# The last feed-forward product of a two-layer trunk: features on the partitions, or tokens

## The chip, the cores and the metric

The kernel runs on one core of one Trainium2 chip. The metric is the device time of one execution in microseconds; lower is better. Five engines work beside each other: TensorE (PE; PEld is its load of the stationary operand), VectorE (DVE), ScalarE (ACT), GpSimd (POOL) and SyncE (SP, which here issues loads and stores). Each runs its own queue in order and waits for others by semaphores.

## What is computed

The reference is a two-layer decoder trunk on x of 256 tokens by 1024 features, all in float32. Cut to what matters here, its end:

```python
h = modulate(rms_norm(x, norm_g[1, 2]), sh3, sc3)
g, u = jnp.split(h @ ffn_w_in[1, 1], 2, axis=-1)          # 1024 -> 2 x 2816
x = x + 0.5 * g3[:, None, :] * ((silu(g) * u) @ ffn_w_out[1, 1])   # 2816 -> 1024
return rms_norm(x, final_g)
```

Ahead of it stand three more such feed-forward blocks, a differential attention and a forgetting attention, which the change leaves alone.

## The kernel before

x lies in SBUF with features on the partitions: tile `xx`, 128 partitions x 8 blocks of features x 256 tokens. Every weight is streamed from memory by SP in pieces of up to 1024 columns into six `raw` buffers; ACT rounds a piece to the matmul's format (`wh`, `cp_part`, line 286), DVE takes the rest (`wl`, `sub_part`, line 296), into six and five buffers. Each product is three matmuls: high by high, low by high, high by low (`mm3`, line 396: the weights are the loaded operand and the activations stream, 256 columns). `v_proj` (line 717) has it the other way round: activations loaded for each half of the tokens, weights streamed, 512 columns.

The order of the work is written out by the program: a planner (`InOrder`, line 55) keeps an estimated clock for each engine, and `bg`, `fill_act` and `fill_dve` put the pieces' casts and subtractions between the other instructions as buffers come free. `later`, `run_laters` and `flush` (lines 381 to 394) put work off by so many steps of the loop.

The block at the end is `ffn(1, 1, "late", ..., None)`. Its first loop over j = 0 to 10 computes 256 hidden features at a time into PSUM banks pg and pu; `evac` makes silu(g) * u and splits it into `hidh` and `hidl`, 22 blocks of 128 features by 256 tokens in all. Its second loop goes over n = 0 to 7, a block of 128 output features each: 22 x 3 matmuls into one bank `po`, then `x_update` (line 417): DVE adds gate times po to x[n], ACT squares it and multiplies it by final_g, and DVE sums the squares over n. After the last n, `rstd_of` (line 446) sums over the partitions with a matrix of ones (two matmuls into psn), takes the reciprocal root on ACT and refines it in three DVE steps; four DVE products scale x, two feature blocks each, and SP and ACT store them in turn (lines 1245 to 1250). The output leaves as 128 x 8 x 256, and the host turns it round. `need` (line 225) makes sure that a column of the conditioning (shift, scale, gate; the `ada` products on DVE) has been computed.

Of the kernel before, what the change touches and what calls it, by code (L numbers as in the profile page):

```python
# [10 lines left out]
F32 = mybir.dt.float32  # L11
# [3 lines left out]
ALU = mybir.AluOpType  # L15
# [31 lines left out]

V_NORM = 0
V_KVN = 48
V_FIN = 56  # L50
V_SUB = 64
V_ADAB = 65

# [51 lines left out]
def trunk(ctx, tc, a, out):  # L105
# [54 lines left out]
    def table(func):  # L160
        act.preload_act_table(func)
# [74 lines left out]
    def add_ffn(l, i):  # L236
        if (l, i) == (0, 0):
            stream.extend((a["win0"][k], K0 * 512, 1024) for k in range(NC))
        n = 2 * (NG - K0 if (l, i) == (0, 0) else NG)
        stream.extend((a["win"][win0_of(l, i) + u], 2048, 1024) for u in range(n))  # L240
        stream.extend((a["wout"][(2 * l + i) * 16 + u], 11 * P, 768) for u in range(16))

    add_ffn(0, 0)
    stream += [(a["wqk"][u], 2048, 1024) for u in range(2)]
# [146 lines left out]
    def flush():  # L391
        for e in laters[:]:
            laters.remove(e)
            e[1]()
# [22 lines left out]
    def x_update(n, ps, gate, nxt, acc_eng):  # L417

        dve.scalar_tensor_tensor(x[n], ps, gate[:, n:n + 1], x[n], op0=ALU.mult, op1=ALU.add)
        hh, hl = hn[n]
        if nxt is not None:
            A = mods[nxt[0]][1]
            act.activation(hh, x[n], AF.Copy, scale=A[:, n:n + 1])
        sq = kp.tile([P, S], F32, tag="sq", name=f"sq{n}")
        act.activation(sq, x[n], AF.Square)
        if nxt is None:
            y = xx
            act.activation(y[:, n], x[n], AF.Copy, scale=vecs[:, V_FIN + n:V_FIN + n + 1])  # L430

        def second():
            if nxt is not None:
                dve.scalar_tensor_tensor(hl, x[n], A[:, n:n + 1], hh.bitcast(F32),
                                         op0=ALU.mult, op1=ALU.subtract)
# [94 lines left out]
    def ffn(l, i, kind, m, nxt, at=2):  # L530
# [93 lines left out]
        for j in range(j0, NG):  # L624
            pg, pu = mmbank(f"pg{j}"), mmbank(f"pu{j}")
            for kh in range(2):
                blk = take("win")
                for kk in range(4):
                    k = kh * 4 + kk
                    for b in range(4):  # L630
                        mm3((pg, pu)[b // 2][:, (b % 2) * 256:(b % 2) * 256 + 256],
                            blk(kk * 512 + b * P), hn[k], k == 0 and b % 2 == 0, k == NC - 1)
                    run_laters()
            evac(pg, pu)
            if (l, i) == (0, 0) and j == K0 + 2:
                constants()
        table(AF.Abs_reciprocal_sqrt)
        gate = (l, 2 if i == 0 else 8)
        for n in range(NC):
            po = mmbank(f"po{n}")[:, :S]  # L640
            if n == NC - NFILL:
                mode[0] = "fill"
            for hf in range(2):
                blk = take("wout")
                for kk in range(11):
                    k = hf * 11 + kk
                    if n == 0 and k == 18:
# [8 lines left out]
            if nxt is not None:  # L656
                need(nxt[0]) if n >= 4 else None
            if n == NC - 1 and nxt is not None:
                need(*nxt)
                shift_cols(nxt)  # L660

            def upd(n=n, po=po):
                f = x_update(n, po, mods[gate][1], nxt, dve)
                later(1, f)
            if n < NC - 1:
                later(1, upd)
            else:
                flush()
                flush()
                upd()  # L670
                flush()

    class OutProj:

# [342 lines left out]
    ffn(0, 1, "late", ((0, 7), (0, 6)), (("kv", 1), ("kv", 0)), at=3)  # L1017


    kT = [cp_.tile([P, 512], F32, name=f"kT{j}") for j in range(4)]  # L1020
    vb = [[cp_.tile([P, 512], F32, name=f"vb{t}{nh}") for nh in range(2)] for t in range(2)]
# [223 lines left out]
    y = xx  # L1245
# [27 lines left out]
def _layout(x, c, ada_w, ada_b, norm_g, ffn_w_in, ffn_w_out, a_w_qkv, a_w_o, a_lambda,  # L1273
# [56 lines left out]
    r["wout"] = ffn_w_out.reshape(4, 2, 11, P, NC, P).transpose(0, 4, 1, 3, 2, 5).reshape(64, P, 11 * P)  # L1330

    def vmat(w):
        return w.reshape(2, 4, P, 2, 512).transpose(3, 0, 2, 1, 4).reshape(4, P, 2048)
# [42 lines left out]
```

## Time and profile before

| | us |
|---|---|
| median of 3 runs | 989.79 (988.62 to 990.39) |
| the profiled execution | 990.28 |
| its span, first to last instruction | 988.5 |
| PE busy | 974.5 (99%) |
| DVE, ACT, POOL busy | 807.1, 561.4, 63.3 |
| first loop of the last block, from about 807; second loop | to 918.49; 918.49 to 978.35 |
| from the last po matmul to the span's end | 10.15 |

The profile is of one execution. A matmul's own duration (0.28) is modelled to its last result; the pace is read from start to start or from the length of a chain of matmuls. Engines' busy shares are averages over stages with different limits, so a stage is read by its own stretch.

### The profile page before, as it was taken

The page shows a single profiled execution, that of the slowest core. Times are in us where ns is not written, and L with a number is a line of the kernel's source. Part 1 is how long each engine was busy: PE and PEld are TensorE (multiplying, and loading weights), DVE is VectorE, ACT ScalarE, POOL GpSimd, SP SyncE. Part 2 cuts the span into 40 slices and gives each one's busy share as a digit, 9 for nine tenths or more (in the row PEclk, how much of TensorE's full clock was granted, in tenths as well). Part 3 has the DMA queues.
Part 4 walks back from the last instruction along what each step waited for, and adds up shares of the span by engine and source line. Part 5 has one row for each costly group of instructions (what it writes and reads, how often), then busy time and mean ns, then how long its engine had stood idle before and what let it go on. Part 6 is the DMA issues. An engine that isn't in the chain of part 4 may idle for free. (4 is left out here: it accounts for less than half of the span.)

```text
span 988.5 us, 20569 instructions
## 1 busy us (share of the span) xinstructions
PE 974.5 (99%) x8168; PEld 949.6 (96%) x8168; DVE 807.1 (82%) x1329; ACT 561.4 (57%) x923; POOL 63.3 (6%) x88
## 2 busy tenths in 40 slices
PE   8999999999999999999999999999999999999996
PEld 7999999988999999999998999999998999999996
DVE  6989879989899998788897988889986697555553
ACT  4465545575877644555575544445567676554552
POOL 0000100000112000000100000000047110000000
PEclk9999999999999999999999999999999999999998
DMA  9987999958766699889957999989765237554551
GB/s 361 414 336 277 338 363 332 364 205 303 271 226 234 227 383 362 302 266 314 337 185 301 342 343 332 331 289 342 256 226 173 84 117 256 197 194 144 176 177 43
DMA packets 67570, 265.07 MB, mean 268 GB/s; under 512 B 7785, under 2 KB 7937, under 8 KB 57362
## 3 DMA queue, kind: packets, MB, share of 16 engines
q1 hardware_dynamic: 65376, 258.31, 72.8%
q0 software_dynamic: 1664, 4.81, 1.7%
q8 instruction: 64, 1.05, 0.4%
q10 hardware_dynamic: 434, 0.64, 0.2%
q14 instruction: 32, 0.26, 0.1%
HBM read 262.66 MB, written 2.65 MB: 268 GB/s over the span
## 5 line engine op out<-in xcount | busy, mean ns | idle before, releaser
L100 DVE TENSOR_TENSOR wl<-raw,wh 128x1024 fp32r<-128x1024 f32 (+1 forms) x368 | 401.6, 1106 | 95.0 <-issue 24.9
L100 ACT CAST wh<-raw 128x1024 fp32r<-128x1024 f32 (+1 forms) x368 | 349.1, 958 | 205.3 <-PE pu L100 98.8
L100 DVE CUSTOM_DVE_ANT_0 ada<-ada,cact,vecs 128x1024 f32<-128x1024 f32 x160 | 203.5, 1279 | 0.2 <-DMA ada<-in_ada 0.2
L100 PE MATMUL po<-hidl,wh 128*128 128x256 f32 x704 | 194.4, 276 | 0.2 <-DVE hidl L100 0.2
L100 PE MATMUL po<-hidh,wh 128*128 128x256 f32 x704 | 194.4, 276 | 0.0
L100 PE MATMUL po<-hidh,wl 128*128 128x256 f32 x704 | 194.3, 276 | 0.0
L100 PE MATMUL pg<-HH,wl 128*128 128x256 f32 x608 | 168.2, 277 | 0.0
L100 PE MATMUL pg<-HH,wh 128*128 128x256 f32 x608 | 168.2, 277 | 0.0
L100 PE MATMUL pu<-HH,wh 128*128 128x256 f32 x608 | 168.1, 277 | 0.0
L100 PE MATMUL pu<-HL,wh 128*128 128x256 f32 x608 | 168.1, 276 | 0.0
L100 PE MATMUL pg<-HL,wh 128*128 128x256 f32 x608 | 168.0, 276 | 0.0
L100 PE MATMUL pu<-HH,wl 128*128 128x256 f32 x608 | 168.0, 276 | 0.0
L100 PEld LDWEIGHTS po<-hidl,wh 128*128 128x128 f32 x704 | 132.1, 188 | 0.4 <-DVE hidl L100 0.4
L100 PEld LDWEIGHTS po<-hidh,wh 128*128 128x128 f32 x704 | 132.2, 188 | 0.0
L100 PEld LDWEIGHTS po<-hidh,wl 128*128 128x128 f32 x704 | 132.2, 188 | 0.0
L100 PEld LDWEIGHTS pg<-HH,wh 128*128 128x128 f32 x608 | 114.1, 188 | 0.7 <-ACT hidh L100 0.6
L100 PEld LDWEIGHTS pg<-HL,wh 128*128 128x128 f32 x608 | 114.2, 188 | 0.0
L100 PEld LDWEIGHTS pg<-HH,wl 128*128 128x128 f32 x608 | 114.2, 188 | 0.0
L100 PEld LDWEIGHTS pu<-HH,wh 128*128 128x128 f32 x608 | 114.2, 188 | 0.0
L100 PEld LDWEIGHTS pu<-HL,wh 128*128 128x128 f32 x608 | 114.2, 188 | 0.0
L100 PEld LDWEIGHTS pu<-HH,wl 128*128 128x128 f32 x608 | 114.2, 188 | 0.0
L100 ACT ACTIVATE HH<-ht,modall 128x256 fp32r<-128x256 f32 x56 | 28.0, 508 | 39.9 <-DVE ht L100 38.0
(215 smaller groups left out, 1627.5 us busy)
## 6 DMA issues: line engine op xcount, KB each, us to landing
raw<-in_win SPq DMA_DIRECT2D x176, 512.0 KB, 6.1
ada<-in_ada SPq DMA_DIRECT2D x79, 1024.0 KB, 7.5
raw<-in_wout SPq DMA_DIRECT2D x64, 384.0 KB, 5.1
raw<-in_wout SPq DMA_DIRECT2D x64, 320.0 KB, 4.7
raw<-in_wqk SPq DMA_DIRECT2D x16, 512.0 KB, 5.4
raw<-in_wo SPq DMA_DIRECT2D x16, 512.0 KB, 5.0
raw<-in_wv SPq DMA_DIRECT2D x8, 512.0 KB, 7.2
raw<-in_wkk SPq DMA_DIRECT2D x8, 512.0 KB, 8.5
```

What stands on the lines that cost most here:

```text
L100: return self.tc.keep_in_program_order(f(*args, **kw))
```

## The change

The second loop of the last block is written anew, with its norm and its stores (class `Last`); the other three blocks keep theirs. Tokens now lie on the partitions. For each quarter of the output features (256), two banks are filled, one for each half of the tokens: `hid` is the loaded operand, 128 tokens wide, and the split weights stream, 256 columns. The weights come from a new array `wlast` with the same numbers in that order, in pieces of 1024 and 768 columns, each at an offset of 32 columns in its buffer. In the last quarter the first eight blocks are done for both halves, then the other fourteen for the first half of the tokens, its update and its store, and then the same for the second half.

So x has to be turned. In the first loop, at j = 1, DVE transposes all of x in squares of 32x32 into the tile `turned`; at j = 2 to 9 POOL issues four DMAs each, 32 in all, that put the squares into place in x's own tile (runs of 32 floats). At j = 6 POOL writes the gate to memory and reads it back as a row on all partitions, and reads final_g likewise. The tiles of the forgetting attention's keys and values are joined into two tiles whose room `turned` and `rows` take over. The sum of squares is now along the free dimension, on DVE with each quarter, and the root is a power on POOL over one column. The output leaves as 128 x 2 x 1024.

```diff
+    shift.update({p: 32 for p, v in enumerate(pieces) if v[0].tensor is a["wlast"].tensor})
...
             evac(pg, pu)
...
+            if nxt is None:
+                last.between(j)
+        if nxt is None:
+            last.down(hid)
+            return
         table(AF.Abs_reciprocal_sqrt)
...
+        def between(self, j):
+            if j == 1:
+                self.turned = cp_.tile([P, NC, 2, 4, 32], F32, tag="kT", name="turned")
+                for k in range(0, NC, 2):
+                    dve.transpose(self.turned[:, k:k + 2].rearrange("p k h b j -> p (k h b j)"),
+                                  xx[:, k:k + 2].rearrange("p k t -> p (k t)"))
+            elif 2 <= j < 10:
+                for fb, tb in self.moves[2 * j - 4:2 * j - 2]:
+                    to = self.x[tb * 32:tb * 32 + 32].rearrange("p h (k b j) -> p h k b j", k=NC, b=4)
+                    for h in range(2):
+                        nc.gpsimd.dma_start(to[:, h, :, fb], self.turned[fb * 32:fb * 32 + 32, :, h, tb])
+            if j == 6:
+                need(self.gate)
+                g = mods[self.gate][1]
+                gdram = tc.dram_tile([1, D], F32, name="gdram")
+                nc.gpsimd.dma_start(bass.AP(gdram.tensor, gdram.offset, [[1, P], [P, NC]]), g)
+                self.rows = cp_.tile([P, 2, D], F32, tag="vb", name="rows")
+                nc.gpsimd.dma_start(self.rows[:, 0], bass.AP(gdram.tensor, gdram.offset, [[0, P], [1, D]]))
+                nc.gpsimd.dma_start(self.rows[:, 1], bass.AP(a["fin"].tensor, a["fin"].offset, [[0, P], [1, D]]))
+
+        def update(self, t, q, po):
+            cs = slice(q * 256, q * 256 + 256)
+            xs = self.x[:, t, cs]
+            m = kp.tile([P, 256], F32, tag="sq", name=f"m{t}{q}")
+            dve.tensor_tensor(m, po, self.rows[:, 0, cs], op=ALU.mult)
+            dve.tensor_tensor(xs, m, xs, op=ALU.add)
+            j = kp.tile([P, 256], F32, tag="ht", name=f"j{t}{q}")
+            s = self.sums[:, 8 * t:8 * t + 8]
+            dve.tensor_tensor_reduce(j, xs, xs, 1.0, 0.0, ALU.mult, ALU.add, accum_out=s[:, q:q + 1])
...
+            elif q == 3:
+                dve.tensor_scalar(s[:, 6:7], s[:, 3:4], 1.0 / D, s[:, 5:6], op0=ALU.mult, op1=ALU.add)
+                nc.gpsimd.tensor_tensor(s[:, 7:8], s[:, 6:7], half[:, :1], op=ALU.pow)
+            if q < 3:
+                dve.tensor_tensor(xs, xs, self.rows[:, 1, cs], op=ALU.mult)
+
+        def store(self, t):
+            r = self.sums[:, 8 * t + 7:8 * t + 8]
+            y = self.x[:, t]
+            act.activation(y[:, :512], y[:, :512], AF.Copy, scale=r)
+            act.dma_start(out[:, t, :512], y[:, :512])
+            dve.scalar_tensor_tensor(y[:, 768:], y[:, 768:], r, self.rows[:, 1, 768:], op0=ALU.mult, op1=ALU.mult)
+            dve.tensor_scalar(y[:, 512:768], y[:, 512:768], r, None, op0=ALU.mult)
+            sp.dma_start(out[:, t, 512:], y[:, 512:])
+
+        def down(self, hid):
+            def part(po, t, k, w):
+                hh, hl = hid[k // 2]
+                o = (k % 2) * 256 + t * P
+                wh, wl = w
+                mm(po, hh[:, o:o + P], wh, start=k == 0, stop=False)
+                mm(po, hh[:, o:o + P], wl, start=False, stop=False)
+                mm(po, hl[:, o:o + P], wh, start=False, stop=k == 21)
+                work(P)
+            mode[0] = "fill"
+            for q in range(4):
+                po = [mmbank(f"po{q}{t}")[:, :256] for t in range(2)]
+                for u in range(3 if q < 3 else 1):
+                    blk = take("wlast")
+                    for kk in range(8 if u < 2 else 6):
+                        k = 8 * u + kk
...
+                        w = blk(kk * 256, 256)
+                        for t in range(2):
+                            part(po[t], t, k, w)
+                        run_laters()
+                if q < 3:
+                    for t in range(2):
+                        later(1 + t, lambda t=t, q=q, po=po: self.update(t, q, po[t]))
+            flush()
+            blks = [take("wlast", True) for _ in range(2)]
+            for t in range(2):
+                for k in range(8, 22):
+                    part(po[t], t, k, blks[(k - 8) // 8](k % 8 * 256, 256))
+                self.update(t, 3, po[t])
+                self.store(t)
...
+    last = Last(1, (1, 8))
     ffn(1, 1, "late", ((1, 7), (1, 6)), None, at=3)
-    y = xx
-    r = rstd_of()
-    rb = r.rearrange("p (o t) -> p o t", o=1).to_broadcast([P, 2, S])
-    for k in range(0, NC, 2):
-        dve.tensor_tensor(y[:, k:k + 2], y[:, k:k + 2], rb, op=ALU.mult)
-        (sp, act)[k // 2 % 2].dma_start(out[:, k:k + 2], y[:, k:k + 2])
...
+    r["wlast"] = w[3].reshape(22, P, 4, 256).transpose(2, 1, 0, 3).reshape(4, P, 22 * 256)
```

## Rows read from the trace of the kernel before

**Rows 1.** The page's busy time by engine, and TensorE's granted clock in 40 slices of the span, in tenths of full speed.

```profile
PE 974.5 (99%) x8168; PEld 949.6 (96%) x8168; DVE 807.1 (82%) x1329; ACT 561.4 (57%) x923; POOL 63.3 (6%) x88
...
PEclk9999999999999999999999999999999999999998
```

**Rows 2.** Busy time by stretch. The columns are the stretch and its length, busy us and instructions of PE, PEld, DVE, ACT and POOL, the granted clock, the DMA share and GB/s. A stretch of an earlier block, the last block's first loop, its second loop, and the end.

```profile
330.00:400.00 70.00, 70.00 (x619) 70.00 (x618) 65.88 (x87) 36.02 (x41) 0.00 (x0) 1.00 0.93 347
...
829.00:918.00 89.00, 89.00 (x788) 89.00 (x787) 48.41 (x49) 43.34 (x50) 0.00 (x0) 1.00 0.56 183
918.50:978.40 59.90, 59.90 (x530) 59.86 (x529) 31.16 (x44) 28.63 (x43) 0.00 (x0) 1.00 0.45 136
978.40:988.50 10.10, 1.06 (x4) 0.30 (x2) 4.29 (x8) 1.40 (x3) 0.00 (x0) 0.66 0.28 104
```

**Rows 3.** The chain that ended last, in order of time, from 915 us on: start, length, engine and tile.

```profile
918.49 59.86 PE po L100 x528
...
978.37 0.49 DVE x L100
...
980.60 0.49 DVE ra L100
...
981.12 0.44 DVE ra L100
...
982.04 0.69 DVE x L100
```

**Rows 4.** The queues of SP and ACT at the end (start, time from the first issue to the end of the last), and the output's tile: issue times in ns, and time from issue to landing.

```profile
982.76 1.58 SPq L100 DMA_DIRECT2D out<-x  x2
983.37 1.61 ACTq L100 DMA_DIRECT2D out<-x  x2
...
L100 ACTq DMA_DIRECT2D out<-x x2: 350/350/350, 983.4 to 984.6; - x2
...
DMA to landing us min/median/max: 2.4/2.5/2.6
```

**Rows 5.** TensorE's pace. The chain from 786 us on: seventy-two pw matmuls of 256 columns, and groups of six of the first loop of the last block at two lengths. Then from TensorE's timeline the first and the last of seventeen rows, each the first of three 512-column matmuls of v_proj.

```profile
788.25 8.57 PE pw L100 x72
...
811.42 0.71 PE pu L100 x6
812.13 0.68 PE pg L100 x6
...
528.40 0.39 PE L100 MATMUL pv<-wh,HH 128*128 128x512 f32 x1
...
539.39 0.39 PE L100 MATMUL pv<-wh,HH 128*128 128x512 f32 x1
```

**Rows 6.** Groups of instructions by line, engine, operation, tiles and shapes: busy us, mean ns of one, idle time before them.

```profile
L100 DVE TENSOR_TENSOR wl<-raw,wh 128x1024 fp32r<-128x1024 f32 x240 | 289.8, 1222 | 57.5 <-issue 19.9 <-ACT sg L100 14.9 <-PE pu L100 10.5
...
L100 DVE CUSTOM_DVE_ANT_0 ada<-ada,cact,vecs 128x1024 f32<-128x1024 f32 x160 | 203.5, 1279 | 0.2 <-DMA ada<-in_ada 0.2
...
L100 ACT ACTIVATE sq<-x 128x256 f32<-128x256 f32 x48 | 19.5, 406 | 14.6 <-DVE x L100 13.7 <-POOL acc L440 1.0
...
L100 DVE SCALAR_TENSOR_TENSOR x<-po,modall,x 128x256 f32<-128x256 f32 x32 | 15.3, 479 | 7.4 <-PE po L100 7.3
...
L100 DVE TENSOR_TENSOR acc<-acc,sq 128x256 f32<-128x256 f32 x20 | 8.4, 421 | 2.4 <-ACT sq L100 2.4
...
L100 DVE CUSTOM_DVE_ANT_0 nl<-s,g 128x256 f32<-128x256 f32 x16 | 6.7, 419 | 0.0
...
L934 POOL TENSOR_TENSOR ss<-ss,half 128x2 f32<-128x2 f32 x8 | 5.6, 700 | 27.3 <-DVE ss L100 26.3 <-DVE rs L100 0.9
...
L100 ACT ACTIVATE x<-x,vecs 128x256 f32<-128x256 f32 x8 | 4.1, 511 | 0.3
...
L100 DVE TENSOR_TENSOR onb<-wb,rsb 128x256 f32<-128x256 f32 x8 | 3.4, 425 | 3.5 <-PE wb L100 3.5
...
L100 DVE TENSOR_SCALAR nl<-nl,rs 128x256 f32<-128x256 f32 x8 | 2.8, 348 | 0.0
...
L100 DVE DVE_READ_ACCUMULATOR2_ANT nm<- 128x1 f32 x32 | 2.6, 83 | 0.0
...
L100 ACT ACTIVATE sqs<-x 128x512 f32<-128x512 f32 x4 | 2.3, 620 | 1.8 <-DMA x<-in_x 1.8
...
L100 DVE TENSOR_SCALAR rs<-rs,small 128x2 f32<-128x2 f32 x8 | 1.8, 230 | 0.3
```

**Rows 7.** Waits between 829 and 918 us (us in total, times, longest), and the tile of the conditioning's products with their first and last start.

```profile
DVE wl L100 <- PE pu L100: 12.2, 8, 1.8
...
L100 DVE CUSTOM_DVE_ANT_0 ada<-ada,cact,vecs x160: 1266/1279/1289, 8.4 to 712.8; 128x1024 f32<-128x1024 f32 x160
```

**Rows 8.** POOL's issues (by form: busy us, mean ns) and landings (KB each, median us); the queues' share of 16 engines between 3 and 7.5 us, and of the whole span for q0.

```profile
L1102 POOL DMA_DIRECT2D fkb<-fdram x8 | 4.6, 579 | 197.7 <-PE po L100 195.6 <-POOL d L1111 1.5 <-PE sb L100 0.3
...
fdram<-fk POOLq DMA_DIRECT2D x1, 16.0 KB, 5.8
...
q10 hardware_dynamic: 144, 0.12, 7.7%
q0 software_dynamic: 32, 0.00, 0.4%
...
q0 software_dynamic: 1664, 4.81, 1.7%
```

More of the change, by code (lines that the diff above doesn't have):

```diff
@@ L49 @@
 V_KVN = 48
-V_FIN = 56
 V_SUB = 64
@@ L240, in add_ffn @@
         stream.extend((a["win"][win0_of(l, i) + u], 2048, 1024) for u in range(n))
-        stream.extend((a["wout"][(2 * l + i) * 16 + u], 11 * P, 768) for u in range(16))
+        if (l, i) == (1, 1):
+            for u in range(4):
+                stream.extend((a["wlast"][u, :, c:c + n], n, step)
+                              for c, n, step in ((0, 2048, 1024), (2048, 2048, 1024), (4096, 1536, 768)))
+        else:
+            stream.extend((a["wout"][(2 * l + i) * 16 + u], 11 * P, 768) for u in range(16))
     add_ffn(0, 0)
@@ L422, in x_update @@
         hh, hl = hn[n]
-        if nxt is not None:
-            A = mods[nxt[0]][1]
-            act.activation(hh, x[n], AF.Copy, scale=A[:, n:n + 1])
+        A = mods[nxt[0]][1]
+        act.activation(hh, x[n], AF.Copy, scale=A[:, n:n + 1])
         sq = kp.tile([P, S], F32, tag="sq", name=f"sq{n}")
         act.activation(sq, x[n], AF.Square)
-        if nxt is None:
-            y = xx
-            act.activation(y[:, n], x[n], AF.Copy, scale=vecs[:, V_FIN + n:V_FIN + n + 1])
         def second():
-            if nxt is not None:
-                dve.scalar_tensor_tensor(hl, x[n], A[:, n:n + 1], hh.bitcast(F32),
-                                         op0=ALU.mult, op1=ALU.subtract)
+            dve.scalar_tensor_tensor(hl, x[n], A[:, n:n + 1], hh.bitcast(F32),
+                                     op0=ALU.mult, op1=ALU.subtract)
             if n == 0:
@@ L655, in ffn @@
             need(gate)
-            if nxt is not None:
-                need(nxt[0]) if n >= 4 else None
-            if n == NC - 1 and nxt is not None:
+            if n >= 4:
+                need(nxt[0])
+            if n == NC - 1:
                 need(*nxt)
@@ L671, in ffn, with __init__ @@
                 flush()
+    class Last:
+        def __init__(self, l, gate):
+            self.l, self.gate = l, gate
+            self.x = xx.rearrange("p k t -> p (k t)").rearrange("p (h d) -> p h d", h=2)
+            self.sums = kp.tile([P, 16], F32, tag="ssl", name="ssl", bufs=1)
+            self.moves = [(fb, tb) for fb in range(4) for tb in range(4)]
+        def between(self, j):
[26 more added lines that the diff above has]
+            dve.tensor_tensor_reduce(j, xs, xs, 1.0, 0.0, ALU.mult, ALU.add, accum_out=s[:, q:q + 1])
+            if q == 1:
+                dve.tensor_tensor(s[:, 4:5], s[:, 0:1], s[:, 1:2], op=ALU.add)
+            elif q == 2:
+                dve.tensor_tensor(s[:, 4:5], s[:, 4:5], s[:, 2:3], op=ALU.add)
+                dve.tensor_scalar(s[:, 5:6], s[:, 4:5], 1.0 / D, EPS, op0=ALU.mult, op1=ALU.add)
+            elif q == 3:
[27 more added lines that the diff above has]
+                        k = 8 * u + kk
+                        if q == 0 and k == 18:
+                            flush()
+                            flush()
+                        w = blk(kk * 256, 256)
[5 more added lines that the diff above has]
+                        later(1 + t, lambda t=t, q=q, po=po: self.update(t, q, po[t]))
+            flush()
+            blks = [take("wlast", True) for _ in range(2)]
[4 more added lines that the diff above has]
+                self.store(t)
@@ L1017, in trunk @@
     ffn(0, 1, "late", ((0, 7), (0, 6)), (("kv", 1), ("kv", 0)), at=3)
-    kT = [cp_.tile([P, 512], F32, name=f"kT{j}") for j in range(4)]
-    vb = [[cp_.tile([P, 512], F32, name=f"vb{t}{nh}") for nh in range(2)] for t in range(2)]
+    kv = [cp_.tile([P, 4, 512], F32, tag=n, name=n) for n in ("kT", "vb")]
+    kT = [kv[0][:, j] for j in range(4)]
+    vb = [[kv[1][:, 2 * t + nh] for nh in range(2)] for t in range(2)]
     fg = kp.tile([P, NC, BH], F32, tag="acc", name="fg", bufs=1)
@@ L1243, in trunk @@
     pace[0] = PACE[6]
+    last = Last(1, (1, 8))
     ffn(1, 1, "late", ((1, 7), (1, 6)), None, at=3)
-    y = xx
-    r = rstd_of()
-    rb = r.rearrange("p (o t) -> p o t", o=1).to_broadcast([P, 2, S])
-    for k in range(0, NC, 2):
-        dve.tensor_tensor(y[:, k:k + 2], y[:, k:k + 2], rb, op=ALU.mult)
-        (sp, act)[k // 2 % 2].dma_start(out[:, k:k + 2], y[:, k:k + 2])
 def _constants():
@@ L1329, in _layout @@
     r["win"] = cat(win, axis=0)
-    r["wout"] = ffn_w_out.reshape(4, 2, 11, P, NC, P).transpose(0, 4, 1, 3, 2, 5).reshape(64, P, 11 * P)
+    w = ffn_w_out.reshape(4, FF, D)
+    r["wout"] = w[:3].reshape(3, 2, 11, P, NC, P).transpose(0, 4, 1, 3, 2, 5).reshape(48, P, 11 * P)
+    r["wlast"] = w[3].reshape(22, P, 4, 256).transpose(2, 1, 0, 3).reshape(4, P, 22 * 256)
+    r["fin"] = final_g.reshape(1, D)
     def vmat(w):
@@ L1369 @@
          for n, v in arrays.items()}
-    out = nc.dram_tensor("out", (P, NC, S), F32, kind="ExternalOutput").ap()
+    out = nc.dram_tensor("out", (P, 2, D), F32, kind="ExternalOutput").ap()
     with tile.TileContext(nc) as tc:
@@ L1374 @@
     y = np.asarray(r.results[0]["out"])
-    return y.transpose(1, 0, 2).reshape(D, S).T.reshape(1, S, D)
+    return y.transpose(1, 0, 2).reshape(1, S, D)
```

## The prediction

> **What bounds the kernel now.** I read the page's busy line and slices first [rows 1]: the reader sees TensorE (PE) busy 99% of the span at full granted clock, every other engine at 82% or less, and only the last slice with a lower clock. So time is saved only where PE works less, or after it has stopped. Next the stretches of the last feed-forward block [rows 2]: from 829 to 978.4 us PE has no idle time, VectorE (DVE) is busy about half the time, ScalarE (ACT) less, GpSimd (POOL) not at all, and the DMA share is 0.45 to 0.56. Then the chain that ended last [rows 3]: one piece of 528 po matmuls, 59.86 us (113.4 ns each), ends at 978.35, and behind it hangs a serial tail: x update, square, the two psn matmuls, root, three DVE steps, four scalings of 0.69, stores. The timeline of that tail [rows 4] shows two issues on ACT's queue that fill 983.37 to 984.98, 0.35 each: the last one starts at 984.63, 6.28 us after PE's end, and the span ends at 988.5, 3.87 us after that. The profiled execution took 990.28 us, 1.78 above its span and 0.49 above the median 989.79; I make the sum against 990.28 and carry the difference over to the median.
>
> **The product itself.** 528 matmuls of 256 moving columns become 4 quarters x 22 blocks x 2 token halves x 3 = 528 of 256 columns: the same count, but hid is now the loaded operand and the split weights stream. If the pace stays 113.4 ns [rows 3] this costs nothing. The trace shows that it need not stay: the pg/pu loop, one and the same code, takes 0.71 us for six in some groups and 0.68 in others, and 72 pw matmuls of 256 columns took 8.57 us, 119.0 ns each, without PE idle [rows 5]. So the ends are 0 and 528 x (119.0 - 113.4) = +3.0 us. The row with the new roles (activations loaded, weights streamed, two token halves) is pv: from 528.40 to 539.39 there are sixteen spans of three 512-column matmuls [rows 5], 10.99 / 48 = 229.0 ns, against 2 x 113.4 = 226.7, 1% more, which is +0.6 here. The po row says 0, the pv row 0.6; I take +0.3, since po is the same stage and width and pv the same roles. The Trainium skill, page "TensorE: Matmul & The Clock Gate", section "Step-by-step: what each phase is for", says that loading the next weights takes no read bandwidth from the running matmul. By that the roles could not matter, the term would be 0 and the sum -2.7; the two paces of rows 5 at full clock speak against it as a law for every stretch.
>
> **Splitting the weights.** 22,528 columns are cast and subtracted before and after, in 24 pieces of 1024 or 768 instead of 32 of 768 or 640: the same columns in fewer instructions. A 1024 piece feeds 24 matmuls, 2.72 us [rows 3], and costs DVE 1.22 [rows 6] and ACT less. Hidden, 0. The updates of quarters 0 to 2 are six times (0.425 + 0.421 + 0.419 + 0.083 + 0.421, and up to 0.25 of small ones), 12 us on DVE, in place of seven x updates and sums of 0.48 + 0.42, 6.3 us; of 59.9 us DVE was busy 31.2 [rows 2], so about 36 then. Cover gone, one token pair of updates (4 us) would be late by at most what the five split buffers do not hold.
>
> **What goes into the loop before.** Four 32x32-square transposes of 128x512 on DVE: no such operation is in the trace; between the 0.69 of a 128x512 operation [rows 3] and the 1.28 of the 128x1024 ada product [rows 6], 2.8 to 5.1 us together; I take 2.8, the row of its size. They are queued ahead of weight subtractions at about 830 us; there DVE waits again and again for PE to free a buffer or for a later instruction [rows 7], so it runs ahead, and the delay costs 0; without that lead up to 5.1. need(gate) at j = 6 finds nothing to do: the last ada product starts at 712.8 [rows 7]. POOL, idle there, issues 32 moves and 3 others; an issue takes 0.58 [rows 8], some 20 us for all, over the 87 of j = 2 to 9. The read of the gate rows waits for the write of the gate to memory, 5.8 us by fdram [rows 8]; behind it on POOL's queue stand the final_g rows and the moves of j = 7 to 9, and the first update that needs them comes some 25 us later (j = 9 is called about 908, quarter 0 ends about 933.5). SP's queue is passed by nothing: its weight loads stay in order.
>
> The 32 moves are 8192 runs of 128 bytes. Bounds per run: 9 ns (32 tiny packets of q0 at 0.4% of 16 engines x 4.5 us) and 38 ns (144 packets of q10 at 7.7%, 0.12 MB) [rows 8]. 8192 / 16 = 512 runs per engine, 4.6 to 19.5 us of an 89 us stretch whose DMA share is 0.56; with 5 to 22 points more it stays under the 0.93 at which 330 to 400 us ran with PE never idle [rows 2]. Cost 0.
>
> **The tail.** Removed with the old one: 6.28 us from PE's end to the last store's issue. The new one, for the second token half (the first half ends 14 x 3 x 113.4 ns = 4.76 us earlier; its update and stores, 3.5 us by the same sum, are over on DVE before that): start 0.02; gate product out of PSUM 0.425 (onb); sum 0.421 (acc); square-and-sum 0.419 + 0.083; one 128x1 scaling 0.23 (rs; 0.17 is the low end); pow on POOL 0.70 (ss); then on DVE 0.48 + 0.35 for the last two quarters [rows 6]; six hand-overs and gaps of 0.03 to 0.06 as between the ra steps [rows 3], 0.3. Together 3.43 us. ACT's half beside it: a scaling of 256 columns takes 0.51, a square of 512 takes 0.21 more than one of 256 [rows 6], so 0.72, ready at 3.3: no later. SP's issue follows at about 3.5 (0.08 as before). So the last issue moves from 6.28 to 3.5: -2.8. The two stores now go together, 512 KB, where they were 0.6 us apart; between 0 (the DMA landed 2.4 to 2.6 us after issue with a neighbour in flight [rows 4]) and 0.7 (256 KB at 375 GB/s); I take 0.1, as those landings already shared. Tail: -2.7, bounds -3.1 (handovers nearly free, 0.17) and -2.0 (0.7 of crowding).
>
> **Sum.** -2.7 + 0.3 = -2.4: 987.9 for an execution like the profiled one, 987.4 for the median.
>
> **The rivals.**
> 1. *The last product runs at the slower pace.* Place: 918.5 to 978.4; price +2.4 (117.9) to +3.0 (119.0), so -0.3 to +0.3 in all: about 989.8. For it: the slow pace stood for 72 matmuls in a row with the same kinds of operand [rows 5]. Against: nothing slows po or most of pg, and pv shows 1%. Chance 0.25.
> 2. *The last quarter outruns its weights.* From its ninth block on, one token half goes through four pieces in 4.76 us instead of 9.5, and the pieces must all be split; if the last two come late, PE stands up to 2.7, one piece: about 990.1, and no gain. Against: DVE and ACT have half their time free [rows 2], and the fifth buffer lets the last piece be split four blocks early. Chance 0.08.
> 3. *Slower: the 128-byte runs crowd out the weight loads* before 918 us. The engines have 0.44 x 89 = 39 us free, and six raw buffers are a lead of 6 x 2.72 = 16 us; it decides from (39 + 16) / 512 = 107 ns a run. At 162 ns (1.7% of 16 engines x 988.5 us over its 1664 packets of q0, mean 2.9 KB [rows 8]) it would be 83 - 55 = +28 us, 1015. Against it: 900-byte packets took 38 ns. Chance 0.04. The Trainium skill, page "DMA: Bandwidth & Descriptors", section "Specifications", says that below 512 B a transfer becomes a read-modify-write; its section "Why small descriptors are slow (HBM only)" excepts moves inside SBUF. Doubling 38 ns gives 77, short of 107; that rule makes me give this 0.04 rather than 0.02.
>
> The forecast, tail shorter by 2 to 3.1 with the pace within 1.2 us of today's, has 0.63: 986.7 to 989.0.
>
> **How the numbers follow.** The measurement of this kernel can tell about 0.2%, 2.0 us, from no change. Of the forecast's 0.63 about 0.07 stays within that, so faster 0.56; rivals 1 and 2 and this part are the same, 0.38; slower is rival 3 and a worst sum of 1 and 2, 0.06. The range holds the forecast and rival 1: from -3.3 (tail bound, pace 0, and a little for the runs' spread) to +0.6 (tail -2.4, pace +3.0): 986.5 to 990.4.
>
> **What would show it.** The po matmuls after: 528 in 59.9 to 60.5 us, six in 0.68; 0.71 is rival 1, an idle gap of PE in the last quarter waiting for wl or wh is rival 2, PE waiting for raw before 918 is rival 3. After the last matmul: three DVE operations of 0.42, POOL once, last issue 3.3 to 3.7 later, end 3.9 behind it. The prediction is wrong above all if the pace shifts, or if the small steps between DVE, POOL and ACT cost more than their rows.

## The result, and the profile after

| | before | after |
|---|---|---|
| median of 20 executions each, taken in turn (us) | 989.47 | 992.34 |
| ratio of after to before, 95% interval | | 1.0026 (1.0014 to 1.0037) |
| the profiled execution; its span | 990.28; 988.5 | 991.55; 989.8 |
| executions from the lowest to the highest | 988.53 to 993.89 | 988.19 to 996.73 |

The change makes the kernel slower, by 0.26% or about 2.6 us by the ratio. One execution on each side that stands hundreds of microseconds above all others (1212 and 1970) is left out of the ratio and of the last row; the medians of the first row, 2.9 us apart, count it, and without it they are 989.33 and 991.55, 2.2 us apart. The after kernel's executions spread more: nine of them lie between 993 and 997, where of before's only one lies above 993.

The profiled execution lost 1.3 us of span, and that is made of three terms. They are read in the order in which the program runs.

**1. Ahead of the last block: +0.8.** The chain of waits of the kernel after, its last group of pu and its piece of po matmuls (start, length, line, count):

```profile
918.60 0.68 PE pu L99 x6
919.28 57.26 PE po L99 x486
```

The po product began at 918.49 before [rows 3] and begins at 919.28 now. Nothing in the first loop of the last block delays it: the stretches of the kernel after (bounds, length, busy time of PE, PEld, DVE, ACT and POOL with instruction counts, granted clock, DMA share, GB/s) show PE busy without a gap from 829 on.

```profile
829.00:919.20 90.20, 90.20 (x798) 90.20 (x797) 50.89 (x50) 44.96 (x50) 15.17 (x27) 1.00 0.72 212
919.20:981.50 62.30, 62.26 (x529) 62.06 (x527) 35.84 (x65) 19.86 (x22) 0.58 (x1) 1.00 0.39 120
981.50:989.80 8.30, 0.00 (x0) 0.00 (x0) 2.25 (x7) 0.72 (x1) 0.56 (x1) 0.67 0.21 79
```

So the loss lies earlier. POOL's timeline from 695 to 737 us, in the forgetting attention, first rows (start, length, line, operation, idle time before it and its releaser):

```profile
714.85 0.96 POOL L703 DMA_DIRECT2D gdram<-modall  x1 [188.47 <-DVE modall L99]
722.23 0.56 POOL L1203 DMA_DIRECT2D fkb<-fdram  x1 [6.42 <-PE po L99]
...
732.37 3.61 POOL L1212 TENSOR_SCALAR d<-fkb,Fq 128x128 f32<-128x128 f32 x4 [8.75 <-DMA fkb<-fdram]
```

The program calls the gate's write at j = 6 of the last block, about 875 us. The queue has it at 714.85, as soon as the gate was computed, and ahead of the loads of `fkb`, the decay rows of the forgetting attention. In the kernel before, the first loads are at 721.74 and 722.56 and the first decay starts at 729.64:

```profile
721.74 0.57 POOL L1102 DMA_DIRECT2D fkb<-fdram  x1 [195.61 <-PE po L100]
729.64 3.73 POOL L1111 TENSOR_SCALAR d<-fkb,Fq 128x128 f32<-128x128 f32 x4 [6.54 <-DMA fkb<-fdram]
```

The DMA view of 714 to 733 us shows what happened on the way. Its first lines are the busy share of the DMA engines in tenths and GB/s, in 40 slices of 0.475 us; then issues by group, with size and median time from issue to landing. The kernel before:

```profile
DMA  9868968999998699985779989997899979985689
GB/s 336 241 207 181 216 207 276 319 259 311 371 414 336 259 336 362 293 224 216 190 172 216 293 328 388 302 276 259 354 414 397 423 293 319 267 293 198 241 354 388
...
raw<-in_wo SPq DMA_DIRECT2D x5, 512.0 KB, 6.6
raw<-in_wq SPq DMA_DIRECT2D x3, 512.0 KB, 5.2
fkb<-fdram POOLq DMA_DIRECT2D x2, 256.0 KB, 8.1
```

and the kernel after:

```profile
DMA  9678898989889999995578459887999979899999
GB/s 371 216 267 259 285 310 241 354 208 224 200 263 312 337 121 69 78 78 78 86 60 121 147 216 207 259 285 310 379 293 259 216 172 233 259 371 405 405 397 405
...
raw<-in_wo SPq DMA_DIRECT2D x5, 512.0 KB, 9.4
raw<-in_wq SPq DMA_DIRECT2D x3, 512.0 KB, 9.8
fkb<-fdram POOLq DMA_DIRECT2D x2, 256.0 KB, 10.2
gdram<-modall POOLq DMA_DIRECT2D x1, 4.0 KB, 11.8
```

For eight slices, 720.6 to 724.4 us, everything together moved 60 to 121 GB/s where the same stretch before never falls under 172; the engines are busy for half of these slices or more, and move little. The 4 KB write takes 11.8 us to land, and the fkb loads and the weights beside it land 2 to 5 us later. A dip alone would not tell: run 4 below, without the write, has one too (86 to 155 GB/s for five slices). The landings tell. In this view the five profiles with the write at this place have 9.4 to 11.8 us for the weights of in_wo and 10.2 to 12.4 for fkb; the nine without it there have 6.0 to 6.8 and 5.4 to 9.3. By the page the Trainium skill titles "DMA: Bandwidth & Descriptors", section "Rules for kernel authors", a last dimension that is not contiguous becomes one descriptor per element; the gate's write is 1024 elements of 4 bytes. The trace does not show that many: queue q0 has 192 packets in this view and 160 in the one of before. Run 11 below tells whether the single elements are the point.

PE pays some 20 us later, where it waits for the decays anyway. Two stretches of the kernel before, columns as above:

```profile
746.00:750.00 4.00, 3.14 (x24) 2.27 (x23) 4.00 (x16) 3.38 (x11) 3.98 (x3) 1.00 0.83 274
750.00:756.00 6.00, 6.00 (x54) 5.54 (x54) 2.74 (x16) 4.15 (x16) 4.17 (x6) 1.00 0.61 224
```

and of the kernel after:

```profile
746.00:750.00 4.00, 2.36 (x20) 1.89 (x20) 3.98 (x12) 3.35 (x10) 3.66 (x5) 1.00 0.78 209
750.00:756.00 6.00, 5.84 (x52) 4.97 (x50) 2.77 (x13) 4.77 (x16) 4.69 (x7) 1.00 0.85 308
```

0.86 + 0.00 us idle became 1.64 + 0.16: +0.94. At 919 the lag is 0.79, and not all of it is the write's. The last ada product, ahead of the write, started at 712.8 before [rows 7] and starts at 713.1 here, so some 0.3 us had been lost earlier, in code that both kernels share:

```profile
L99 DVE CUSTOM_DVE_ANT_0 ada<-ada,cact,vecs x160: 1267/1278/1286, 8.4 to 713.1; 128x1024 f32<-128x1024 f32 x160
```

**2. The last product: +2.4.** 486 matmuls took 57.26 us in the chain, 117.8 ns each, where 528 took 59.86, 113.4 ns each [rows 3]. From start to start over all 528 the paces are 117.8 and 113.3 ns, a difference of 4.45, and 528 x 4.45 = +2.35.

**3. The tail: -1.8.** From 10.15 us to 8.34. The timeline of the kernel after from 980 to 990 us, its last rows:

```profile
981.18 0.28 PE L99 MATMUL po<-wh,hidl 128*128 128x256 f32 x1
981.50 0.42 DVE L99 TENSOR_TENSOR m<-po,rows 128x256 f32<-128x256 f32 x1 [1.90 <-PE po L99]
981.96 0.43 DVE L99 TENSOR_TENSOR x<-m,x 128x256 f32<-128x256 f32 x1
982.42 0.43 DVE L99 CUSTOM_DVE_ANT_0 j<-x 128x256 f32<-128x256 f32 x1
982.77 0.08 DVE L99 DVE_READ_ACCUMULATOR2_ANT ssl<- 128x1 f32 x1
982.89 0.21 DVE L99 TENSOR_SCALAR ssl<-ssl 128x1 f32<-128x1 f32 x1
983.18 0.56 POOL L725 TENSOR_TENSOR ssl<-ssl,half 128x1 f32<-128x1 f32 x1 [4.37 <-DVE ssl L99]
983.77 0.72 ACT L99 ACTIVATE x<-x,ssl 128x512 f32<-128x512 f32 x1 [4.20 <-POOL ssl L725]
983.77 0.48 DVE L99 SCALAR_TENSOR_TENSOR x<-x,ssl,rows 128x256 f32<-128x256 f32 x1 [0.67 <-POOL ssl L725]
984.18 0.35 DVE L99 TENSOR_SCALAR x<-x,ssl 128x256 f32<-128x256 f32 x1
984.53 0.38 ACTq L99 DMA_DIRECT2D out<-x  x1
984.55 0.34 SPq L99 DMA_DIRECT2D out<-x  x1
```

The last matmul ends at 981.46 and the last issue starts at 984.55, 3.09 us later (6.28 before). But from there to the end of the span it is 5.25 us, where it was 3.87. The instructions of the program's last line (queue, operation, count: shortest, median and longest in ns, first and last start) name what ends last:

```profile
L1470 POOLq DRAIN  x3: 46/102/5833, 983.1 to 989.5; - x3
L1470 SPq DRAIN  x3: 7/7/7, 987.9 to 989.2; - x3
```

POOL's closing drain starts at 983.1, before the power, and lasts 5.83 us, to about 988.9, while SP saw the stores landed and came to its drain at 987.9. So of the 5.25 about 1 us is POOL's.

-1.81 + 2.35 + 0.79 = +1.33, against 1.3 of span. This execution lies in the middle of its set: nine are shorter, nine are longer, by up to 5 us. The experiments say what they can of the longer ones.

### The profile page after: what moved, and what is told of

Same layout as the page of the kernel before. It is cut to its first block, busy times and chain, and to the rows that moved or that the text cites. A ratio compares the mean times of both kernels' runs of the same rounds, so it can differ in the third digit from the quotient of the medians.

```text
span 989.8 us, 20567 instructions
## 1 busy us (share of the span) xinstructions
PE 975.2 (99%) x8164; PEld 951.3 (96%) x8164; DVE 812.9 (82%) x1354; ACT 552.3 (56%) x899; POOL 85.0 (9%) x125
## 5 line engine op out<-in xcount | busy, mean ns | idle before, releaser
L99 PE MATMUL po<-hidh,wh 128*128 128x256 f32 x528 | 145.7, 276 | 0.0
L99 PE MATMUL po<-hidh,wl 128*128 128x256 f32 x528 | 145.7, 276 | 0.0
L99 PE MATMUL po<-hidl,wh 128*128 128x256 f32 x528 | 145.7, 276 | 0.0
L99 PEld LDWEIGHTS po<-hidh,wh 128*128 128x128 f32 x528 | 99.1, 188 | 0.0
L99 PEld LDWEIGHTS po<-hidh,wl 128*128 128x128 f32 x528 | 99.1, 188 | 0.0
L99 PEld LDWEIGHTS po<-hidl,wh 128*128 128x128 f32 x528 | 99.1, 188 | 0.0
```

The source lines that it names most:

```text
L99: return self.tc.keep_in_program_order(f(*args, **kw))
```

## The experiments

Theory: three separate terms, namely the gate's write in the attention, the pace of the last product, and a tail whose gain is partly given back to POOL. Rivals: a single cause for all of it (the clock, or the moves of x), and for each term a cause of its own, named at the run. Of each run one execution was profiled, and the last four columns are of that one. The start of the first decay also moves with what came earlier: in these profiles the last ada product, ahead of the write, starts between 711.5 and 714.9 us. The wait for fkb just before that decay (8.75 us in the kernel after, 6.54 in the kernel before) does not have that part. Before took 989.69, 989.82 and 989.66 us (medians of 30 to 35 executions) beside runs 1 to 4, 5 to 8 and 9 to 12.

| run | median (us) | ratio to before, 95% | span | ns per po matmul | first decay starts | its wait for fkb |
|---|---|---|---|---|---|---|
| 1 after_again | 993.86 | 1.0026 (1.0010 to 1.0043) | 992.4 | 117.8 | 731.96 | 9.07 |
| 2 root_on_act | 993.04 | 1.0016 (1.0000 to 1.0033) | 992.2 | 117.8 | 733.34 | 9.76 |
| 3 shift0 | 989.81 | 0.9991 (0.9971 to 1.0011) | 986.5 | 113.3 | 732.24 | 9.45 |
| 4 before_pool_last | 989.50 | 0.9994 (0.9980 to 1.0007) | 987.5 | 113.3 | 728.26 | 6.45 |
| 5 gate_late | 990.13 | 1.0005 (0.9996 to 1.0015) | 990.0 | 117.8 | 730.68 | 8.03 |
| 6 gate_late_shift0 | 988.21 | 0.9989 (0.9980 to 0.9997) | 988.5 | 113.3 | 730.92 | 5.72 |
| 7 gate_late_shift0_act | 986.76 | 0.9968 (0.9956 to 0.9980) | 985.0 | 113.3 | 729.30 | 6.77 |
| 8 before_gate_write | 993.83 | 1.0037 (1.0021 to 1.0053) | 996.3 | 113.3 | 734.79 | 10.80 |
| 9 best_shift16 | 990.57 | 1.0006 (0.9996 to 1.0017) | 988.0 | 118.7 | 728.12 | 5.82 |
| 10 best_shift32 | 989.51 | 0.9996 (0.9985 to 1.0008) | 990.6 | 117.8 | 728.73 | 6.38 |
| 11 before_gate_row | 989.63 | 0.9997 (0.9986 to 1.0008) | 989.7 | 113.3 | 731.10 | 6.28 |
| 12 double_moves | 986.87 | 0.9974 (0.9960 to 0.9988) | 985.1 | 113.3 | 729.10 | 6.14 |

**1. The kernel after, unchanged**, to have its spread beside the others.

> The changed kernel once more, for the spread of its executions (988.2 to 996.7 us so far, with a gap between about 990 and 993) and for a second profile. Theory 1, the pace of the last product differs from execution to execution: a profile at 113.4 ns a po matmul would end near 987.4 us of span, one at 117.8 near 989.8, and a third pace of about 122 would make the group near 994. Theory 2, POOL's closing drain differs: the po pace stays and the time from the last store's issue to the span's end moves (5.27 us in the first profile, 3.87 before the change). Rival 3 of the prediction, weights held up before 918 us: PE idle there, which the first profile does not show.

993.86. Its profile shows an execution of the longer kind: the same pace and tail as in the first profile, but the last product starts near 921.9, 3.4 us later than before. The same two stretches as above, of this run:

```profile
746.00:750.00 4.00, 2.24 (x15) 1.38 (x13) 3.98 (x12) 3.35 (x12) 3.66 (x5) 0.91 0.77 237
750.00:756.00 6.00, 6.00 (x29) 5.74 (x28) 2.06 (x12) 3.28 (x10) 4.07 (x7) 0.50 0.81 278
```

After the pause the granted clock falls to 0.50, its lower level of 1.2 GHz, and PE gets through 29 matmuls in 6 us instead of 54. This is where this execution loses. The fall is not the early write's alone. With the write early, the stretch 750 to 756 shows 0.50 in runs 1 and 2, 0.73 in run 8, and 1.00 in the first profile and run 3; without it there, it shows 0.74 in run 5, 0.50 in run 10, and 1.00 in before and the other six. Every execution's mean granted clock is on record, and the five with a fall there have 0.993 or 0.994, the nine others 0.995 or more. By that mark 21 of 67 executions with the early write are low, 9 of 82 of the runs without it, and 11 of 100 of before beside them: the write makes the fall more frequent. It does not explain all of the longer executions. Of the 18 of this kernel (both sets) above 993 us, nine are at 0.995 or 0.996; where those lose is not shown.

**2. The root on ACT.** The power on POOL becomes ACT's reciprocal root and three DVE steps that refine it, with the table loaded at the start of the last product:

```diff
-                nc.gpsimd.tensor_tensor(s[:, 7:8], s[:, 6:7], half[:, :1], op=ALU.pow)
+                act.activation(s[:, 3:4], s[:, 6:7], AF.Abs_reciprocal_sqrt)
+                dve.scalar_tensor_tensor(s[:, 4:5], s[:, 6:7], s[:, 3:4], s[:, 3:4], op0=ALU.mult, op1=ALU.mult)
+                dve.tensor_scalar(s[:, 5:6], s[:, 4:5], -0.5, 1.5, op0=ALU.mult, op1=ALU.add)
+                dve.tensor_scalar(s[:, 7:8], s[:, 5:6], s[:, 3:4], None, op0=ALU.mult)
...
+            table(AF.Abs_reciprocal_sqrt)
```

> The changed kernel with the last root on ACT and three small DVE steps in place of POOL's power. If POOL's closing drain (5.8 us from the last power, ending 1.1 us after SP is done) sets the end, the time from the last store's issue to the span's end falls from 5.27 to about 3.9 and the median falls by 1.0 to 1.2 us less the longer root (about 0.2). If the group of executions near 994 us is also POOL's drain, it disappears and the spread becomes that of the kernel before. If the drain only fills time that DMA needs anyway: no change.

993.04; beside the 993.86 of run 1 the median cannot tell a gain of this size. The profile can: POOL's drain now stands right behind its last moves, from 854.9 us on, and from the last matmul's end to the end of the span it takes 7.55 us (984.65 to 992.2) in place of 8.34, although the root is three instructions longer. The executions near 994 us stay (989.65 to 996.4 in all), so POOL's drain does not make them.

**3. Offset 0.** The pieces of `wlast` start at column 0 of their buffers:

```diff
-    shift.update({p: 32 for p, v in enumerate(pieces) if v[0].tensor is a["wlast"].tensor})
+    shift.update({p: 0 for p, v in enumerate(pieces) if v[0].tensor is a["wlast"].tensor})
```

> The changed kernel with the pieces of the last product's weights at the start of their buffers, not 32 columns in. If the pace of the po matmuls (117.8 ns in the first profile against 113.4 before the change) hangs on where the streamed operand lies, it moves: 113.4 would give 2.4 us back, 119 to 122 would cost 0.6 to 2.2 more. If the pace hangs on the roles of the operands alone, it stays at 117.8 and the median at about 992.

989.81, 4.05 below run 1 beside it, and 113.3 ns per matmul. The pace alone is worth 2.4; the executions of this kernel lie in two clusters (986.9 to 988.4 and 991.2 to 995.5, six each), so the rest is how many fell in which.

**4. Before, with one power on POOL at the very end.** Nothing uses its result.

```diff
+    nc.gpsimd.tensor_tensor(small[:, 12:13], y[:, 7, :1], half[:, :1], op=ALU.pow)
```

> The kernel before with one more POOL power over one column of the scaled x, behind everything else; its result is not used. Theory 2: POOL's drain lasts about 5.2 us from the end of its last operation whatever else runs; that operation would end near 985.2 us, the drain near 990.4, so the span grows by about 2.7 us. If the drain only waits for the stores, the span stays within 0.3 us of 988.5.

989.50, no difference, and from the last po matmul to the end of the span it is 10.2 us as before; the drain that follows the late power lasts 2.98 us and not the 5.8 of the kernel after. The theory that any late work of POOL costs a drain of fixed length fell here. In its place I supposed that the drain grows with the number of DMAs that POOL has issued (28 here, 63 after); run 12 is for that.

**5. The gate's write at j = 6.** DVE copies the gate into spare columns at j = 6, and the write takes it from the copy, so that it cannot be queued sooner:

```diff
-                g = mods[self.gate][1]
+                g = self.sums[:, 16:]
+                dve.tensor_copy(g, mods[self.gate][1])
```

> The changed kernel with the gate copied by DVE into another tile at j = 6 of the last block, and written to memory from that copy, so that the write can't stand ahead of the fkb loads on POOL's queue in the forgetting attention. Theory 3: that write delays the first fkb loads (landing seen at 732.0 to 732.4 us where it was 729.6 before the change), PE idles longer around 746 to 749 and in the slow executions drops to 1.2 GHz until about 756. Then the fkb landing goes back to about 729.6, the offset at the end of that attention (+0.8 and +3.5 us in the two profiles) to within 0.5 us of 0, and the group near 994 us disappears: median about 989.9, that is 989.5 - 1.8 (tail) + 2.4 (pace). Rival: these pauses come from the phases of the executions and not from the write: spread and median stay at 988 to 997 and 992 to 994.

990.13: by the ratios to before, 1.0005 against 1.0026 twice, 2.1 us below the kernel after, and nothing lies above 992.61. The write is issued at 874.89. Two details came out otherwise than expected. The first decay starts at 730.68 and not at about 729.6, its wait of 8.03 us being shorter than with the early write but longer than before's 6.54. And the po product begins at 919.55, 1.06 after before's and not within 0.5, in an execution whose granted clock fell:

```profile
750.00:756.00 6.00, 6.00 (x41) 5.54 (x40) 1.14 (x5) 3.02 (x11) 3.65 (x6) 0.74 0.62 227
```

The traffic stands still at the new place as well; the DMA view of 874 to 893 us:

```profile
GB/s 388 181 43 190 241 241 303 135 44 78 336 310 129 26 26 17 17 0 0 17 78 60 35 17 26 43 9 17 43 190 328 250 121 147 198 276 336 345 431 371
...
raw<-in_win SPq DMA_DIRECT2D x7, 512.0 KB, 9.9
```

For 16 slices, 880.2 to 887.8 us, it is 0 to 78 GB/s, and the weights land after 9.9 us (4.2 in this stretch of the kernel after). But the fkb loads are long over, and PE is busy 30.00 of 30.00 us from 875 to 905: there the pieces already loaded cover it.

**6 and 7. Late write and offset 0; and the root on ACT as well.** Their edits are those of runs 5, 3 and 2.

> The same with the streamed weights at the start of their buffers. If the three terms add up (tail -1.8, pace 0, attention 0): median about 987.6 with few executions over 990. If the pace at shift 0 was an accident of one profile: the po matmuls at 117.8 ns again and about 990.

> The same with the last root on ACT and DVE. The tail was 7.55 us with it and 8.32 to 8.34 without: median about 986.8, which is the forecast of the prediction less its pace term.

988.21 and 986.76, where 987.6 and 986.8 were expected; in run 6 two of eleven executions lie above 990. The three terms add: run 7 has none of the three losses, is faster than both kernels, and its executions (six) lie within 986.24 to 987.46. Its last matmul ends at 977.47, its last issue starts at 980.84, and the span ends at 985.0: a tail of 7.53, of which 4.16 after the issue.

**8. The write alone, in the kernel before.** The gate is written to memory on POOL's queue as in the change, nothing reads it, and the rest is the kernel before:

```diff
+    need((1, 8))
+    gdram = tc.dram_tile([1, D], F32, name="gdram")
+    nc.gpsimd.dma_start(bass.AP(gdram.tensor, gdram.offset, [[1, P], [P, NC]]), mods[(1, 8)][1])
```

> The kernel before with one part of the change alone: the gate's write to memory on POOL's queue, which comes ahead of the fkb loads as in the changed kernel; nothing reads it. Theory 3: fkb lands some 2.4 us later, the forgetting attention ends 0.8 to 3.7 us later, and most executions fall into the group near 993: median 990.5 to 993. Rival (the pauses come from elsewhere in the change): median within 0.5 us of 989.7.

993.83, 4.0 above before. POOL's timeline, first rows from 695 us:

```profile
715.25 0.96 POOL L1246 DMA_DIRECT2D gdram<-modall  x1 [188.46 <-DVE modall L100]
722.62 0.55 POOL L1102 DMA_DIRECT2D fkb<-fdram  x1 [6.42 <-PE po L100]
...
734.79 2.63 POOL L1111 TENSOR_SCALAR d<-fkb,Fq 128x128 f32<-128x128 f32 x3 [10.80 <-DMA fkb<-fdram]
```

The wait for fkb is 10.80 us where it was 6.54. One 4 KB write costs as much as the whole change. It is more than the 990.5 to 993 expected. The profile shows the longest of its twelve executions (998.22), so the sizes in it are not typical.

**9 and 10. Run 7 with other offsets**, 16 and 32 columns.

> The version with late gate copy, offset 0 and the root on ACT took 986.76 us at 113.3 ns per matmul of the last product; here the pieces of wlast lie 16 columns into their buffers. Theory 'any offset slows the streamed weights': 117.8 ns, +2.4 us, 989.1. Theory 'only where an offset of 32 moves the operand into another spot; 16 is what the pg/pu pieces use and half of those groups run at 0.68': 113.3 ns, 986.8. Something between, such as 115.5 ns and 988.0, would say that the cost grows with the offset.

> The same with the offset of 32 columns that the change has. Theory 'the offset alone sets the pace, whatever else the kernel does': 117.8 ns per matmul and 986.76 + 2.4 = 989.1 us. Rival 'the pace came with something else that the other two edits took away': 113.3 ns and 986.8.

The chains' pieces of po, of run 9, of run 10 and of run 7:

```profile
917.79 62.66 PE po L99 x528
```

```profile
920.86 62.20 PE po L99 x528
```

```profile
917.62 59.85 PE po L99 x528
```

118.7, 117.8 and 113.4 ns. Any offset tried slows the streamed weights, and the larger one does not slow them more; both of the other thoughts, that 16 is harmless and that the cost grows with the offset, fell. The medians, 990.57 and 989.51, are 3.8 and 2.75 above run 7's, of which the pace is 2.8 and 2.35.

**11. Run 8 with runs of 32 bytes.** Each partition writes its eight values side by side, 128 runs in place of 1024 elements; the order in memory is then not the row that the change needs, and nothing reads it.

```diff
-    nc.gpsimd.dma_start(bass.AP(gdram.tensor, gdram.offset, [[1, P], [P, NC]]), mods[(1, 8)][1])
+    nc.gpsimd.dma_start(bass.AP(gdram.tensor, gdram.offset, [[NC, P], [1, NC]]), mods[(1, 8)][1])
```

> The kernel before with the gate written to memory on POOL's queue ahead of the fkb loads, as in the run where that took 993.83 us, but each partition writes its 8 values as one run of 32 bytes: 128 runs in place of 1024 elements (their order in memory is then not the row that the change needs; nothing reads them here). Theory 'it is the number of elements that holds up the loads queued behind it': the first decay that uses fkb starts at about 729.7 as in the kernel before, and the median is 989.7. Rival 'any transfer put ahead of the fkb loads costs this, by its issue and its place': the first decay stays at 732 to 735 and the median at 992.5 to 994.

989.63, as before. POOL's timeline, and from the DMA view of 714 to 733 us the write's landing:

```profile
716.07 0.57 POOL L1246 DMA_DIRECT2D gdram<-modall  x1 [188.48 <-DVE modall L100]
...
731.10 3.74 POOL L1111 TENSOR_SCALAR d<-fkb,Fq 128x128 f32<-128x128 f32 x4 [6.28 <-DMA fkb<-fdram]
```

```profile
gdram<-modall POOLq DMA_DIRECT2D x1, 4.0 KB, 4.2
```

At the same place in the queue the same 4 KB land in 4.2 us instead of 11.8 to 13.9, and the wait for fkb is 6.28. The first decay starts at 731.10, between the two theories, but here the last ada product already started 1.5 us later than before (714.3), and the wait is as before. So it is the single elements that cost, not a transfer at that place. What about them costs is not separated: in run 8 neighbouring partitions write neighbouring 4-byte places of memory, in run 11 each partition has 32 bytes of its own, and q0 has 192 packets in the view of run 11 as in that of the kernel after.

**12. Every move of x issued twice**, in run 6's kernel: 95 DMAs on POOL's queue.

```diff
                         nc.gpsimd.dma_start(to[:, h, :, fb], self.turned[fb * 32:fb * 32 + 32, :, h, tb])
+                        nc.gpsimd.dma_start(to[:, h, :, fb], self.turned[fb * 32:fb * 32 + 32, :, h, tb])
```

> The version with late gate copy and offset 0 (root on POOL; 988.21 us) with every one of the 32 moves of x issued twice, so 95 DMAs on POOL's queue in place of 63; the second copy writes the same values. Theory 'POOL's closing drain grows with the DMAs that POOL has issued' (2.4 us after its last operation with 28 or 29 of them, 5.24 with 63, so some 0.08 each): 5.24 + 32 x 0.08 = 7.9 us, and as the drain ends last, the span's end moves by +2.6: about 990.8. Rival 'the drain is longer for another reason, such as the kind of transfer or the late power': 5.2 us and about 988.2. The added moves themselves (18 us of issues on an idle POOL) cost nothing by either.

986.87, lower than run 6 (though the intervals of the two ratios overlap), and neither theory held: the drain became shorter.

```profile
L1472 POOLq DRAIN  x3: 46/102/2892, 979.5 to 984.8; - x3
L1472 SPq DRAIN  x3: 7/7/7, 984.3 to 984.6; - x3
```

2.89 us with 95 DMAs, 5.83 with 63, 2.98 with 28: the count does not set it. With the short drain SP's stores end last, and the span ends 4.15 us after the last issue (980.95), as in run 7 (4.16), so what the long one costs is 5.25 - 4.15 = 1.1 us. What makes it long stays open. The added moves cost nothing.

## Why the prediction was wrong, step by step

It forecast -2.4, faster. It is +2.2 to +2.9 by the medians of the two (and +4.2 in run 1). In the profiled execution the forecast's terms stand so: tail -2.7 against -1.8; pace +0.3 against +2.4; a term for the attention is absent from the sum, and is +0.8 there, some 0.5 of it the write's, and 3.4 in run 1. What failed first is that absent term. With the write late (run 5) the same kernel takes 990.13, close to the 989.8 at which rival 1 stood; only the early write takes it beyond 991.

- **"I take +0.3, since po is the same stage and width and pv the same roles": wrong in size, as rival 1 had it.** The rows of before had both paces in them, and the price of the rival (117.9) is the one that came. What set it was in the diff's first line, the offset of 32 columns, to which the prediction gave no thought: at offset 0 the new roles run at 113.3, just as the old. So the roles cost nothing, and the offset 2.4. The Trainium skill, page "TensorE: Matmul & The Clock Gate", section "Wait — 56ns, not 53.3ns?", gives columns / 2.4 GHz plus about 2.5 ns from start to start and has no term for where the operand begins. An estimate from it is 109.2 ns for 256 columns. The runs measure 113.3, 117.8 and 118.7 at full granted clock, so the measurement decides, and the place counts. Why pw ran at 119.0 [rows 5] isn't answered by this.
- **"need(gate) at j = 6 finds nothing to do" and "SP's queue is passed by nothing": the step that failed.** Both are true as they stand, but the write was taken to be queued where the program calls it. Its input was ready after 712.8 [rows 7], and there POOL's queue has it, ahead of the loads of fkb, which the prediction passed over. The prediction costed the write by fdram's 5.8 us [rows 8], 16 KB; the row's single elements took 11.8 us for 4 KB, and other transfers landed later beside them. Runs 5, 8 and 11 show the links: moved late, PE does not wait for it; put alone into before it costs 4.0; and in runs of 32 bytes nothing.
- **The tail: mechanism right, one term missing.** The last issue comes 3.09 us after the last matmul, for which the sum said 3.5: the power took 0.56 and not 0.70, the closing steps overlap (0.48 and 0.35 start 0.41 apart), and hand-overs are short. The two stores together cost 4.15 - 3.87 = 0.3, between the bounds 0 and 0.7, where 0.1 was taken. What was missing is POOL's closing drain, 1.1 us, which no row of before showed on the path: there POOL was done at about 800 us (its drain starts at 797.3).
- **Splitting and updates: right.** DVE was busy 35.84 us in the last product, where "about 36" was said; the prediction's own terms, 31.2 - 6.3 + 12, give 36.9, so the agreement to a tenth is luck. PE was busy 62.26 of 62.30 us there, so rival 2 did not come.
- **Transposes, moves and rival 3: right in cost.** The rows of the tile `turned` in the kernel after, and POOL's queue in its DMA view of 825 to 860 us:

```profile
L698 POOL DMA_DIRECT2D x<-turned x32: 582/582/635, 825.7 to 851.3; - x32
L99 DVE STREAM_TRANSPOSE turned<-x x4: 668/670/705, 822.9 to 824.7; 128x512 f32<-128x512 f32 x4
```

```profile
q0 software_dynamic: 1024, 1.05, 13.7%
```

The four transposes took 2.7 us, the low bound taken. The 32 issues took 0.58 each as by [rows 8], though back to back and not over eight steps of the loop. Their 8192 runs went as 1024 packets, 0.137 x 16 x 35 us / 1024 = 75 ns each on average, 4.8 us per engine, near the low end (4.6). The DMA share rose from 0.56 to 0.72, and PE had no gap.

With the offset at 0, the write late and the root on ACT the same change gives 986.76, against 987.4 forecast: the gain seen in the tail was real, and two of the three losses came from lines that the sum had at nothing.

## What to carry to other kernels

An instruction is costed where its queue will hold it, not where the program calls it: once its inputs are ready early it can stand ahead of other work, so ask what is then behind it, above all for a DMA that moves single elements. A write of scattered 4-byte values is small in bytes and large in what it holds up; let each run be as long as the layout allows, or tie it to something late. An offset or a slice of a streamed operand is a part of the change like any other, worth one run by itself at offset 0.

## What was not expected of the hardware

- TensorE at full granted clock streamed 256 columns in 113.3 ns at offset 0, in 118.7 at 16 and in 117.8 at 32 columns, with all else the same.
- While a 4 KB write of 1024 single elements was under way, all DMA traffic fell to 60 to 121 GB/s for nearly 4 us in the first profile (0 to 78 for 7.6 us in run 5). It took 11.8 to 13.9 us to land early and 10.3 in run 5; the same bytes in 128 runs took 4.2.
- Behind a late power, POOL's closing drain took 5.83 us in the five profiles with 63 DMAs on its queue, and 2.9 to 3.0 in one each with 28 and with 95; the cause is open.
- A pause in which PE was idle for 1.8 of 4 us (746 to 750, run 1) was followed by 6 us at the lower clock in that execution, while one of 1.6 in the first profile was not. In run 5 the idle time of these 4 us was 0.86, as long as before's, and the clock fell all the same (0.74 in the 6 us that followed).
